# A decoder layer on one core: the last piece's residual in PSUM, transposes in a row, weights first, 4 KB store rows

## The chip, the core and the metric

The kernel runs on one core of a Trainium2 chip. A core has five engines with a queue of instructions each, executed in order: TensorE (PE; matmuls, written to PSUM; a matmul's stationary operand is loaded by a separate step, shown as PEld), VectorE (DVE), ScalarE (ACT), GpSimd (POOL), and SyncE (SP), which only issues DMA transfers here. The engines wait for each other through semaphores. Sixteen DMA engines move data between HBM and SBUF; the queues of SP and ACT feed them. The metric is the time of one execution on the device in microseconds.

## The reference, cut to what matters

One hybrid decoder layer in float32, batch 1, 256 positions, width 2048: retention and an RG-LRU side by side with a gated merge, cross-attention to 256 memory tokens, a gated feed-forward part with a causal convolution, a last RMSNorm. The parts that the change touches:

```python
h = h + memory_cross_attention(hn, mem_n, xa_w_q, xa_w_k, xa_w_v, xa_w_o)   # ends with o @ xa_w_o
hn = rmsnorm(h, norm_ffn_w)
h = h + conv_gated_ffn(hn, ffn_w_up, ffn_conv_w, ffn_conv_b, ffn_w_down)    # silu(gate) * val @ ffn_w_down, width 5632
return rmsnorm(h, final_norm_w)          # y * rsqrt(mean(y*y) + 1e-6) * w
```

Every matrix product is done with float32 operands split into a high part `hi` (float32r, rounded) and a low part `lo` (the rest), as hi*hi + lo*hi + hi*lo, so three matmuls stand for one.

## The kernel before

**Gemms.** All weights lie in one array, `wall`, in the order in which they are used. A gemm makes 512 output columns (a block, `b`) for all 256 rows. Its weights come in chunks of four 128-row tiles, 1 MB each (512 KB for the first ones: `EARLY`, sizes 2, 2, 4, 4, 4 for the first two gemms, which take turns). `prefetch` (L237) asks for the next chunk (a DMA by `load`, L191, at L192) into one of three raw buffers and records its split: `hi` by ACT (L283; by DVE, L281, for the very first piece), `lo` by DVE (L284), in halves of two tiles (`KH`), for the first two pieces in single tiles. `chunks` (L296) takes a chunk from the list `ahead` and calls `prefetch(AHEAD)`, which fills the list up to two. Each chunk of four tiles is 24 matmuls (two row blocks `tt` x four tiles x three products) through `mm` (L222). The activations `s` of the first gemms come from `x_t` through the class `Pairs` (ACT L429, DVE L430).

**Order.** The program is recorded by a framework that schedules each engine's queue by priorities and puts in the semaphores. Matmuls stay in the order of the program; a DMA that is "pinned" (`tc.keep_in_program_order`) does too. A tile that is written waits for those who still use it.

**Turning a block.** After a gemm, a block is turned by DMA (`by_dma`, L364): ACT copies the words into two 16-bit planes `pl` (L372), one for each `tt`; SP issues a transposing DMA for each into `pt` (L373); later ACT joins the halves into `f` (L383), and `split_cols` makes from it the operands `s` of the next gemm. `residual` (L792) does this for the four blocks of `w_mix_out` and of `xa_w_o`: residual add into `hrow[b]` (L804), turning, and sums of squares (L822). After `xa_w_o` comes the first gemm of the feed-forward part, whose last chunk needs the turned block 3.

**The end.** `down` (L949) runs the last gemms with `ffn_w_down`: blocks 0 to 2 as above, each finished by `finish` (squares into `ss3` by ACT, product with the norm weight by DVE). Block 3 is `last_down` (L964), per row block `tt` of 128 rows. For `tt` = 0 it is one sum of 512 columns, for `tt` = 1 two sums of 256 columns, `c` = 0 and 1 (36 matmuls each); they use two PSUM tiles, `accs[0]` and `accs[1]`. Each half is added to the residual (L989), squared and summed by DVE (L991). To have only one column left at the end, the sum of what is known after `c` = 0 (L996, L997) goes through a power of 0.5 on POOL (L998) into column 512 of `last`, behind the half `c` = 1, and is squared with it. A second power, of -0.5, gives the row's scale `r` (L1000). Then ACT and DVE scale the four blocks (L1008, L1004, L1010), and four stores of 128 rows x 2 KB go out (L1012), three by SP's queue, one by ACT's. `WARM` (L35) is the number of matmuls on constants before the first weights arrive (L219).

Of the kernel before, what the change touches and what calls it, by code (L numbers as in the profile page):

```python
# [17 lines left out]
P = 128  # L18
# [15 lines left out]
AHEAD = 2  # L34
WARM = 8  # L35
FREE = 300
# [9 lines left out]
C_INVF, C_SIGN, C_DEC = 0, 1, 2  # L46
C_WIDTH = C_DEC + HEADS * S


def constants():  # L50
# [8 lines left out]
    for h in range(HEADS):  # L59
        lg = np.log1p(-(2.0 ** (-5.0 - h)))  # L60
        dec = np.where(rel >= 0, np.exp(lg * np.maximum(rel, 0.0)), 0.0) * DK**-0.5
        c[:, C_DEC + h * S : C_DEC + (h + 1) * S] = dec
    return c

# [72 lines left out]
def hybrid_layer(  # L137
# [98 lines left out]

    def prefetch(n):  # L237
        while len(ahead) < n and taken[0] < len(stream):
# [13 lines left out]
            cuts = range(nk + 1) if i == 0 else range(0, nk + 1, KH) if i < 6 else (0, nk)  # L252
            if own:
                xs.load(k2 + 1)
            for a, b in zip(cuts, cuts[1:]):
                load(raw[:, a:b, :], src[:, a:b, :], early)
                if i == 0 and a == 0:
                    load(*xs.rest, early)
                elif own and a == 0:
                    xs.load(k2 + nk // KH)  # L260
# [12 lines left out]
            for k in range(0, nk, KH):  # L273
# [3 lines left out]
                lo = wp.tile([P, KH, BW], F32R, tag="lo", bufs=PART_BUFS, name=nm("lo"))  # L277
                for cs in (slice(k, k + 1), slice(k + 1, k + 2)) if i < 2 else (slice(k, k + KH),):
                    ds = slice(cs.start - k, cs.stop - k)
# [16 lines left out]
    def chunks(nk, w, row, c):  # L296
# [4 lines left out]
        for k, n in pieces(i, nk):  # L301
            prefetch(1)
            (r_, c_), parts = ahead.pop(0)
            assert (r_, c_) == (row + k * P, c)
            prefetch(AHEAD)
            yield k, n, parts
            step[0] += 1
            due = [p for p in pending if p[0] <= step[0]]
            pending[:] = [p for p in pending if p[0] > step[0]]
            for _, fn in due:  # L310
                fn()
# [51 lines left out]

    def by_dma(rows, then, wait=1):  # L364

# [4 lines left out]
        for tt in range(2):  # L370
            with tc.high_priority(FREE):
                act.copy(planes[:, tt], words[:, tt])  # L372
            sp.dma_start_transpose(  # L373
                out=turned_.rearrange("p h f s -> p (h f) s")[:, :, tt * P : (tt + 1) * P],
                in_=planes[:, tt].rearrange("p h n -> p (h n)"),
            )

        def join():
# [413 lines left out]
    def residual(w, st, out, wcol, steps=None):  # L792
# [3 lines left out]
        for b in range(4):  # L796
            if steps:
                steps(b)
            if b == 0:
                for one in products[:2]:  # L800
                    for _ in range(NT // KC - 1):
                        next(one)
            h = hrow[b]
            dve.tensor_add(h, h, ended(products[b]))  # L804
            by_dma(h, lambda f, b=b: turn(f, b, out, wcol), 1 + (b == 1))
            if b < 2:
# [157 lines left out]
    def last_down(b0, hid, n, b):  # L964
# [3 lines left out]
        dve.memset(half, 0.5)  # L968
        accs = [acc(), acc()]
        parts = [p for _, _, ps in chunks(n, "ffn_w_down", b0 * BW, b * BW) for p in ps]  # L970

        def total(o, tt, cs):
            for k in range(n):
                hi, lo = (t[:, k % KH, cs] for t in parts[k // KH])
                for _ in products_n(o, hid[k // 2][:, k % 2, :], hi, lo, tt, k == 0, k == n - 1):
                    pass

        for tt in range(2):
# [4 lines left out]
            for c in range(2):  # L983
                cs = slice(c * S, (c + 1) * S)
                o = accs[c][:, 1, 0:S] if tt else accs[0][:, 0, cs]
                if tt:
                    total(o, tt, cs)
                y = last[:, c * S : (c + 1) * S + c]
                dve.tensor_add(last[:, cs], h[:, tt, cs], o)  # L989
                junk = tp.tile([P, S + 1], F32, tag="tr", bufs=2, name=nm("junk"))  # L990
                dve.scalar_tensor_tensor(  # L991
                    out=junk[:, 0 : S + c], in0=y, scalar=1.0 / D if c else 1.0, in1=y, op0=ALU.mult, op1=ALU.mult,
                    accum_out=ss3[:, tt, b + c : b + c + 1],
                )
                if c == 0:
                    dve.tensor_reduce(out=before, in_=ss3[:, tt, 0:4], axis=AX.X, op=ALU.add)  # L996
                    dve.tensor_scalar_add(before, before, EPS * D)  # L997
                    pool.tensor_tensor(out=last[:, BW : BW + 1], in0=before, in1=half, op=ALU.pow)  # L998
            r = sp_.tile([P, 1], F32, tag="ro", bufs=5, name=nm("ro"))
            pool.tensor_tensor(out=r, in0=ss3[:, tt, 4:5], in1=mhalf[:, 0:1], op=ALU.pow)  # L1000
            for c in (1, 0, 3, 2):
                y = hrow[c][:, tt, :]
                if c == 3:
                    dve.scalar_tensor_tensor(  # L1004
                        out=y, in0=last[:, 0:BW], scalar=r, in1=wfin[1][:, 1, :], op0=ALU.mult, op1=ALU.mult
                    )
                elif c == 1:
                    dve.tensor_scalar_mul(y, y, r)  # L1008
                else:
                    act.mul(y, y, r)  # L1010
                queue = act if c == 2 else sp
                queue.dma_start(out=out[0, tt * P : (tt + 1) * P, c * BW : (c + 1) * BW], in_=y)  # L1012

# [10 lines left out]
    for kind, b, *n in ff_plan():  # L1024
# [6 lines left out]
        else:  # L1031
            final = b + n[0] == NF // 4
            if final:
                wfin = []
                for i in range(2):
# [40 lines left out]
```

## Time and profile before

| | us |
|---|---|
| three runs: lowest, median, highest | 2005.92, 2006.1, 2006.18 |
| the profiled execution: its time | 2006.16 |
| its span, first to last instruction | 2004.2 |
| PE busy in the span | 1993.6 |
| ACT busy, DVE busy | 1270.2, 1268.9 |
| DMA queue of SP: share of the 16 engines' span | 64.3% |

The span is what the views count in; the execution's time is 1.96 us longer. A row of a view gives the start, the time, the engine, the line of the kernel, the operation, what is written and from what (with partitions x elements), how many, and in brackets how long the engine was idle before it and who released it. Matmuls overlap in the pipeline: two rows of "0.39" can start 0.23 apart. A merged row ("x2", "x574") goes from the first start to the last end. SPq and ACTq are the issuing of a DMA; "to landing" is from the start of the issue to the last byte's arrival.

### The profile page before, as it was taken

The numbers are of one execution on the slowest core, as the hardware profiler recorded it, in microseconds if no ns is written. First come the engines' busy times: TensorE is split into PE (matmuls) and PEld (weight loads), VectorE is DVE, ScalarE is ACT, GpSimd is POOL, SyncE is SP. The second block draws the span as 40 slices with busy tenths as digits, with TensorE's granted clock in tenths as the row PEclk, the third lists the DMA queues.
The fourth block names the chain that finished last, engine by engine and source line by source line (L and its number), as shares of the span: only waits on it lengthen the run. The fifth ranks groups of instructions, "written<-read, shape, count | busy, mean of one in ns | idle before, by whom it ended". The sixth has DMA issues, their size and how long they took to land.

```text
span 2004.2 us, 23312 instructions
## 1 busy us (share of the span) xinstructions
PE 1993.6 (99%) x8924; PEld 1656.2 (83%) x8924; DVE 1268.9 (63%) x1566; ACT 1270.2 (63%) x1499; POOL 8.8 (0%) x14
## 2 busy tenths in 40 slices
PE   9999999999999999999999999999999999999998
PEld 7888888888888888888888888888888888888887
DVE  6857756888545555566555654667764576754775
ACT  6646548988444555587666666767763577734763
POOL 0000000000000000000000000000000000000000
PEclk9999999999999999999999999999999999999999
DMA  8755657665655556777666567767665577655673
GB/s 328 238 209 172 237 200 206 214 210 179 218 199 192 199 198 212 268 256 241 203 217 211 193 198 206 213 202 226 231 212 194 179 227 229 204 207 202 205 239 119
DMA packets 197904, 425.58 MB, mean 212 GB/s; under 512 B 142240, under 2 KB 146848, under 8 KB 152736
## 3 DMA queue, kind: packets, MB, share of 16 engines
q1 hardware_dynamic: 197360, 423.55, 64.3%
q8 instruction: 70, 1.15, 0.2%
q10 hardware_dynamic: 432, 0.53, 0.1%
q14 instruction: 42, 0.34, 0.0%
HBM read 388.39 MB, written 2.10 MB: 195 GB/s over the span
## 4 chain that ended last, share of the span: by engine, by line
PE 98%; DMA 1%; DVE 0%; ACT 0%; issue 0%; SPq 0%; POOLq 0%; POOL 0%
PE acc L222 96%; PE sm L222 2%; DMA pt<-pl 0%; DMA raw<-in_wall 0%; DVE lo L284 0%; ACT hi L283 0%; SPq L192 0%; ACT pl L372 0%; ACT nat L1010 0%; DVE last L989 0%; DVE nat L804 0%; ACT junk L822 0%; POOLq L1072 0%; POOL last L998 0%; DVE junk L991 0%
## 5 line engine op out<-in xcount | busy, mean ns | idle before, releaser
L222 PE MATMUL acc<-hi,s 128*128 128x512 f32 x5720 | 1757.7, 389 | 1.2 <-DVE last L989 0.8
L222 PEld LDWEIGHTS acc<-hi,s 128*128 128x128 f32 x5720 | 1071.7, 188 | 222.0 <-DVE last L989 1.3
L284 DVE TENSOR_TENSOR lo<-raw,hi 128x1024 fp32r<-128x1024 f32 (+1 forms) x714 | 859.7, 1220 | 596.9 <-ACT hi L283 579.4
L222 PE MATMUL acc<-lo,s 128*128 128x512 f32 x2860 | 1110.0, 388 | 0.5 <-DVE lo L284 0.5
L283 ACT CAST hi<-raw 128x1024 fp32r<-128x1024 f32 (+1 forms) x712 | 734.5, 1050 | 469.4 <-PE acc L222 427.3
L222 PEld LDWEIGHTS acc<-lo,s 128*128 128x128 f32 x2860 | 537.0, 188 | 112.1 <-DVE lo L284 1.3
L383 ACT COPY f<-pt 128x1024 uint16<-128x1024 uint16 x128 | 168.9, 1353 | 99.9 <-DMA pt<-pl 99.9
L372 ACT COPY pl<-rows 128x1024 uint16<-128x1024 uint16 x100 | 99.7, 1045 | 55.2 <-DVE rows L396 42.9
L396 DVE TENSOR_SCALAR rows<-acc,ro 128x512 f32<-128x512 f32 x76 | 53.4, 744 | 6.2 <-PE acc L222 6.2
L917 DVE SCALAR_TENSOR_TENSOR fg<-f,pf,fg 128x255 f32<-128x255 f32 (+1 forms) x88 | 37.4, 479 | 29.7 <-ACT fg L915 29.3
L917 DVE SCALAR_TENSOR_TENSOR fv<-f,pf,fv 128x255 f32<-128x255 f32 (+1 forms) x88 | 36.1, 478 | 3.9 <-ACT fv L915 3.8
L915 ACT ACTIVATE fg<-f,pf 128x256 f32<-128x256 f32 x44 | 22.9, 592 | 0.3
L915 ACT ACTIVATE fv<-f,pf 128x256 f32<-128x256 f32 x44 | 23.1, 592 | 0.0
L729 DVE SCALAR_TENSOR_TENSOR xr<-f,pa,xr 128x255 f32<-128x255 f32 (+2 forms) x48 | 20.2, 480 | 3.4 <-ACT xr L727 3.3
L404 DVE TENSOR_TENSOR s<-f,s 128x512 fp32r<-128x512 f32 x24 | 15.5, 687 | 9.9 <-ACT s L403 9.9
L430 DVE SCALAR_TENSOR_TENSOR s<-f,pb,s 128x256 fp32r<-128x256 f32 x48 | 20.1, 480 | 2.2 <-ACT s L429 2.2
L372 ACT COPY pl<-nat 128x1024 uint16<-128x1024 uint16 x16 | 15.9, 1045 | 7.5 <-DVE nat L804 7.5
L429 ACT ACTIVATE s<-f,pb 128x256 fp32r<-128x256 f32 x48 | 20.6, 503 | 0.0
L222 PEld LDWEIGHTS sm<-s,s 128*128 128x128 f32 x144 | 18.8, 191 | 0.9
L222 PE MATMUL sm<-s,s 128*128 128x256 f32 (+1 forms) x144 | 18.6, 279 | 0.0
L935 ACT ACTIVATE ft<-fg 128x512 f32<-128x512 f32 x22 | 13.9, 632 | 7.3 <-DVE fg L917 7.3
L418 ACT ACTIVATE v<-acc,ro 128x512 fp32r<-128x512 f32 x16 | 11.0, 686 | 10.2 <-DVE v L419 10.2
(137 smaller groups left out, 561.3 us busy)
## 6 DMA issues: line engine op xcount, KB each, us to landing
raw<-in_wall SPq DMA_DIRECT2D x352, 1024.0 KB, 4.9
nat<-in_x SPq DMA_DIRECT2D x8, 512.0 KB, 8.7
raw<-in_wall SPq DMA_DIRECT2D x7, 512.0 KB, 8.6
pt<-pl SPq DMA_TRANSPOSE x128, 3.3
nat<-in_mem SPq DMA_DIRECT2D x4, 512.0 KB, 8.4
xt<-in_x_t SPq DMA_DIRECT2D x3, 512.0 KB, 10.2
xt<-in_mem_t SPq DMA_DIRECT2D x3, 512.0 KB, 4.9
out<-nat SPq DMA_DIRECT2D x6, 256.0 KB, 2.9
```

What stands on the lines that cost most here:

```text
L222: tc.keep_in_program_order(pe.matmul(*a, **k))
L283: act.copy(hi[:, ds], raw[:, cs, :])
L284: dve.tensor_tensor(out=lo[:, ds], in0=raw[:, cs, :], in1=hi[:, ds].bitcast(F32), op=ALU.subtract)
L372: act.copy(planes[:, tt], words[:, tt])
L383: act.copy(halves_[:, :, :, cs], turned_[:, :, :, cs])
L396: dve.tensor_scalar_mul(rows[:, tt, :], a[:, tt, :], r[:, tt : tt + 1])
L404: dve.tensor_tensor(out=t[:, :, S:BW], in0=src, in1=t[:, :, 0:S].bitcast(F32), op=ALU.subtract)
L429: act.activation(t[:, j, 0:S], src[:, j, :], AF.Identity, scale=wcol(j))
L430: dve.scalar_tensor_tensor(out=t[:, j, S:BW], in0=src[:, j, :], scalar=wcol(j), in1=t[:, j, 0:S].bitcast(F32), op0=ALU.mult, op1=ALU.subtract,
L729: dve.scalar_tensor_tensor(out=y[:, s:S], in0=z[:, 0 : S - s], scalar=p_cw(3 - s, t), in1=y[:, s:S], op0=ALU.mult, op1=ALU.add,)
L915: act.activation(y, z[:, j, :], AF.Identity, scale=pf[:, 2, t : t + 1], bias=pf[:, 3, t : t + 1])
L917: dve.scalar_tensor_tensor(out=y[:, s:S], in0=z[:, j, 0 : S - s], scalar=pf[:, 2 - s, t : t + 1], in1=y[:, s:S], op0=ALU.mult, op1=ALU.add,)
```

## The change

The edits:

- the first weight piece is asked for ahead of the first tiles of `x_t`; `WARM` goes from 8 to 7; pieces three and four are split in single tiles, as the first two were;
- for the last block of `xa_w_o` (`hold`), the first three chunks are multiplied first; while the last chunk is taken, `held` keeps `chunks` from calling `prefetch`; both transposes are pinned; then `prefetch(AHEAD, True)` asks for the next chunk, pinned;
- the constants get an identity matrix, loaded ahead of the last part and copied to `one`; the half `c` = 1 of `tt` = 1 of the residual is split into `known` (high and low part), and two matmuls add it to the sum in PSUM ahead of the 36 others (`more`);
- this half's square comes from PSUM by ACT with the sum of squares, over 257 columns: the known sum's root is copied by ACT into column 256 of the same PSUM tile, ahead of that tile's matmuls in the program;
- three PSUM tiles instead of two, so that each sum has its own;
- the product with the norm weight is done for each half of block 3 by DVE (from PSUM for the last), ahead of the scaling;
- scaled blocks are written side by side in pairs into a raw buffer; two stores per row block, with rows of 4 KB, both by SP.

```diff
--- before.py
+++ after.py
@@ -32,7 +32,7 @@
 RAW_BUFS = 3
 PART_BUFS = 6
 AHEAD = 2
-WARM = 8
+WARM = 7
 FREE = 300
 RG_WAIT = 3
 EPS = 1e-6
@@ -44,7 +44,8 @@
 O_XR, O_YR, O_GA, O_GB = 6144, 8192, 10240, 12288
 
 C_INVF, C_SIGN, C_DEC = 0, 1, 2
-C_WIDTH = C_DEC + HEADS * S
+C_ID = C_DEC + HEADS * S
+C_WIDTH = C_ID + P
 
 
 def constants():
@@ -60,6 +61,7 @@
         lg = np.log1p(-(2.0 ** (-5.0 - h)))
         dec = np.where(rel >= 0, np.exp(lg * np.maximum(rel, 0.0)), 0.0) * DK**-0.5
         c[:, C_DEC + h * S : C_DEC + (h + 1) * S] = dec
+    c[:, C_ID:] = np.eye(P)
     return c
 
 
@@ -234,7 +236,9 @@
 
     at = [0]
 
-    def prefetch(n):
+    held = [False]
+
+    def prefetch(n, pin=False):
         while len(ahead) < n and taken[0] < len(stream):
             i = taken[0]
             name, row, nk, c = stream[i]
@@ -250,11 +254,12 @@
             early = i < 2 * len(EARLY)
             own = early and i % 2 == 0
             cuts = range(nk + 1) if i == 0 else range(0, nk + 1, KH) if i < 6 else (0, nk)
-            if own:
+            if own and i > 0:
                 xs.load(k2 + 1)
             for a, b in zip(cuts, cuts[1:]):
-                load(raw[:, a:b, :], src[:, a:b, :], early)
+                load(raw[:, a:b, :], src[:, a:b, :], early or pin)
                 if i == 0 and a == 0:
+                    xs.load(1)
                     load(*xs.rest, early)
                 elif own and a == 0:
                     xs.load(k2 + nk // KH)
@@ -275,7 +280,7 @@
                     xs[k2 + k // KH]
                 hi = wp.tile([P, KH, BW], F32R, tag="hi", bufs=PART_BUFS, name=nm("hi"))
                 lo = wp.tile([P, KH, BW], F32R, tag="lo", bufs=PART_BUFS, name=nm("lo"))
-                for cs in (slice(k, k + 1), slice(k + 1, k + 2)) if i < 2 else (slice(k, k + KH),):
+                for cs in (slice(k, k + 1), slice(k + 1, k + 2)) if i < 4 else (slice(k, k + KH),):
                     ds = slice(cs.start - k, cs.stop - k)
                     if i == 0:
                         dve.tensor_copy(hi[:, ds], raw[:, cs, :])
@@ -302,7 +307,8 @@
             prefetch(1)
             (r_, c_), parts = ahead.pop(0)
             assert (r_, c_) == (row + k * P, c)
-            prefetch(AHEAD)
+            if not held[0]:
+                prefetch(AHEAD)
             yield k, n, parts
             step[0] += 1
             due = [p for p in pending if p[0] <= step[0]]
@@ -361,7 +367,7 @@
 
         return t[:, j, cs], t[:, j, S + cs.start : S + cs.stop]
 
-    def by_dma(rows, then, wait=1):
+    def by_dma(rows, then, wait=1, pin=False):
 
 
         planes = big([P, 2, 2, BW], U16, s="pl")
@@ -370,10 +376,12 @@
         for tt in range(2):
             with tc.high_priority(FREE):
                 act.copy(planes[:, tt], words[:, tt])
-            sp.dma_start_transpose(
+            turning = sp.dma_start_transpose(
                 out=turned_.rearrange("p h f s -> p (h f) s")[:, :, tt * P : (tt + 1) * P],
                 in_=planes[:, tt].rearrange("p h n -> p (h n)"),
             )
+            if pin:
+                tc.keep_in_program_order(turning)
 
         def join():
             f = big([P, 4, S], s="f")
@@ -801,8 +809,16 @@
                     for _ in range(NT // KC - 1):
                         next(one)
             h = hrow[b]
+            hold = b == 3 and steps is None
+            if hold:
+                for _ in range(NT // KC - 1):
+                    next(products[b])
+            held[0] = hold
             dve.tensor_add(h, h, ended(products[b]))
-            by_dma(h, lambda f, b=b: turn(f, b, out, wcol), 1 + (b == 1))
+            by_dma(h, lambda f, b=b: turn(f, b, out, wcol), 1 + (b == 1), hold)
+            if hold:
+                held[0] = False
+                prefetch(AHEAD, True)
             if b < 2:
                 later(2 + b, lambda h=h, b=b: squares(h, ss, b))
             else:
@@ -966,13 +982,22 @@
         h = hrow[b]
         half = sp_.tile([P, 1], F32, tag="half", bufs=1, name="half")
         dve.memset(half, 0.5)
-        accs = [acc(), acc()]
+        accs = [acc() for _ in range(3)]
+        one = tp.tile([P, P], F32R, tag="tr", bufs=2, name="one")
+        dve.tensor_copy(one, unit[0][:, 0, 0:P])
+        rest = h[:, 1, S:BW]
+        known = big([P, 2, S], F32R, s="h")
+        act.copy(known[:, 0, :], rest)
+        dve.tensor_tensor(out=known[:, 1, :], in0=rest, in1=known[:, 0, :].bitcast(F32), op=ALU.subtract)
         parts = [p for _, _, ps in chunks(n, "ffn_w_down", b0 * BW, b * BW) for p in ps]
 
-        def total(o, tt, cs):
+        def total(o, tt, cs, more=False):
+            if more:
+                for i in range(2):
+                    mm(o, one, known[:, i, :], start=i == 0, stop=False)
             for k in range(n):
                 hi, lo = (t[:, k % KH, cs] for t in parts[k // KH])
-                for _ in products_n(o, hid[k // 2][:, k % 2, :], hi, lo, tt, k == 0, k == n - 1):
+                for _ in products_n(o, hid[k // 2][:, k % 2, :], hi, lo, tt, k == 0 and not more, k == n - 1):
                     pass
 
         for tt in range(2):
@@ -982,34 +1007,45 @@
                 total(accs[0][:, 0, :], tt, slice(0, BW))
             for c in range(2):
                 cs = slice(c * S, (c + 1) * S)
-                o = accs[c][:, 1, 0:S] if tt else accs[0][:, 0, cs]
+                o = accs[1 + c][:, 0, 0:S] if tt else accs[0][:, 0, cs]
                 if tt:
-                    total(o, tt, cs)
-                y = last[:, c * S : (c + 1) * S + c]
-                dve.tensor_add(last[:, cs], h[:, tt, cs], o)
+                    total(o, tt, cs, c == 1)
+                if tt and c:
+                    y, z = accs[2][:, 0, 0 : S + 1], o
+                else:
+                    y, z = last[:, c * S : (c + 1) * S + c], last[:, cs]
+                    dve.tensor_add(z, h[:, tt, cs], o)
                 junk = tp.tile([P, S + 1], F32, tag="tr", bufs=2, name=nm("junk"))
-                dve.scalar_tensor_tensor(
-                    out=junk[:, 0 : S + c], in0=y, scalar=1.0 / D if c else 1.0, in1=y, op0=ALU.mult, op1=ALU.mult,
-                    accum_out=ss3[:, tt, b + c : b + c + 1],
-                )
+                if tt and c:
+                    act.activation(
+                        junk, y, AF.Square, scale=float(D**-0.5), accum_out=ss3[:, tt, b + c : b + c + 1]
+                    )
+                else:
+                    dve.scalar_tensor_tensor(
+                        out=junk[:, 0 : S + c], in0=y, scalar=1.0 / D if c else 1.0, in1=y, op0=ALU.mult, op1=ALU.mult,
+                        accum_out=ss3[:, tt, b + c : b + c + 1],
+                    )
                 if c == 0:
                     dve.tensor_reduce(out=before, in_=ss3[:, tt, 0:4], axis=AX.X, op=ALU.add)
                     dve.tensor_scalar_add(before, before, EPS * D)
                     pool.tensor_tensor(out=last[:, BW : BW + 1], in0=before, in1=half, op=ALU.pow)
+                    if tt:
+                        act.copy(accs[2][:, 0, S : S + 1], last[:, BW : BW + 1])
+                dve.tensor_tensor(out=last[:, cs], in0=z, in1=wfin[1][:, 1, cs], op=ALU.mult)
             r = sp_.tile([P, 1], F32, tag="ro", bufs=5, name=nm("ro"))
             pool.tensor_tensor(out=r, in0=ss3[:, tt, 4:5], in1=mhalf[:, 0:1], op=ALU.pow)
-            for c in (1, 0, 3, 2):
-                y = hrow[c][:, tt, :]
-                if c == 3:
-                    dve.scalar_tensor_tensor(
-                        out=y, in0=last[:, 0:BW], scalar=r, in1=wfin[1][:, 1, :], op0=ALU.mult, op1=ALU.mult
-                    )
-                elif c == 1:
-                    dve.tensor_scalar_mul(y, y, r)
-                else:
-                    act.mul(y, y, r)
-                queue = act if c == 2 else sp
-                queue.dma_start(out=out[0, tt * P : (tt + 1) * P, c * BW : (c + 1) * BW], in_=y)
+            scaled = wp.tile([P, 4, BW], F32, tag="raw", bufs=RAW_BUFS, name=nm("out"))
+            rows = [hrow[c][:, tt, :] for c in range(3)] + [last[:, 0:BW]]
+            for c in range(2):
+                dve.tensor_scalar_mul(scaled[:, 2 * c, :], rows[2 * c], r)
+                late = S if c else 0
+                act.mul(scaled[:, 2 * c + 1, late:], rows[2 * c + 1][:, late:], r)
+                if late:
+                    dve.tensor_scalar_mul(scaled[:, 3, 0:late], rows[3][:, 0:late], r)
+                sp.dma_start(
+                    out=out[0, tt * P : (tt + 1) * P, 2 * c * BW : 2 * (c + 1) * BW],
+                    in_=scaled[:, 2 * c : 2 * c + 2, :].rearrange("p c n -> p (c n)"),
+                )
 
     ss3 = sp_.tile([P, 2, 5], F32, tag="ss3", bufs=1, name="ss3")
 
@@ -1031,7 +1067,8 @@
         else:
             final = b + n[0] == NF // 4
             if final:
-                wfin = []
+                wfin, unit = [], [tmp("unit")]
+                sp.dma_start(out=unit[0][:, 0, 0:P], in_=consts[:, C_ID:])
                 for i in range(2):
                     t = big([P, 2, BW], s="wf")
                     sp.dma_start(
```

## The prediction

> **What bounds the kernel now.** I read the page first, then what TensorE (PE) waited for, then the chain of work that ended last.
>
> ```profile
> span 2004.2 us, 23312 instructions
> PE 1993.6 (99%) x8924; PEld 1656.2 (83%) x8924; DVE 1268.9 (63%) x1566; ACT 1270.2 (63%) x1499; POOL 8.8 (0%) x14
> ...
> PE warm L219 <- DVE half L968: 1.1, 1, 1.1
> PE acc L222 <- DVE last L989: 0.8, 1, 0.8
> PE acc L222 <- DVE lo L284: 0.5, 1, 0.5
> PE acc L222 <- DVE s L430: 0.4, 1, 0.4
> ```
>
> PE is idle for 2004.2 - 1993.6 = 10.6 us: 1.1 before its first matmul, three waits (0.8, 0.5, 0.4), and the rest, 7.8 us, after its last matmul. Nothing else can be gained without removing matmuls. The change goes at all three waits and at the tail. The price of a late matmul is read from the chain:
>
> ```profile
> 9.90 1.06 ACT hi L283
> ...
> 12.27 130.41 PE acc L222 x574
> ...
> 1987.45 4.58 PE acc L222 x36
> ```
>
> 574 matmuls of 512 columns in 130.41 us are 0.227 us each; 36 of 256 columns in 4.58 us are 0.12 each, with some 0.1 to fill the pipeline after a stop. Between the stops PE never waits, so what makes it stop costs its full length. Times below are on the clock of this execution, before any shift.
>
> **The start.** These rows stand around the first wait.
>
> ```profile
> 4.73 1.77 PE L222 MATMUL acc<-hi,s 128*128 128x512 f32 x4
> 6.34 0.62 PE L222 MATMUL acc<-lo,s 128*128 128x512 f32 x2
> 7.24 1.15 ACT L283 CAST hi<-raw 128x512 fp32r<-128x512 f32 x2 [2.32 <-DMA raw<-in_wall]
> 7.90 1.29 DVE L284 TENSOR_TENSOR lo<-raw,hi 128x512 fp32r<-128x512 f32 x2 [0.77 <-ACT hi L283]
> 10.98 2.48 DVE L284 TENSOR_TENSOR lo<-raw,hi 128x1024 fp32r<-128x1024 f32 x2 [0.96 <-ACT hi L283]
> 11.04 0.70 PE L222 MATMUL acc<-hi,s 128*128 128x512 f32 x2
> 12.27 0.50 PE L222 MATMUL acc<-lo,s 128*128 128x512 f32 x1 [0.53 <-DVE lo L284]
> ```
>
> The third weight piece lands at 9.9; ACT casts its whole 128x1024 half (1.06), DVE subtracts it (1.24), and PE's first lo matmul, due at 11.04 + 2 x 0.227 = 11.50, starts at 12.27. The change does the third and fourth pieces in 128x512 steps (0.57 ACT, 0.65 DVE by the 7.24 and 7.90 rows): 9.90 + 0.57 + 0.65 = 11.1, before 11.50. The wait of 0.77 goes, and with it 0.1 of refill: -0.9. What is late next is the second half, ready at about 11.8 and due at 12.2. Weights first and one warm matmul less move only what comes before 7.24: the second product's piece lands in the same place of the queue behind the same bytes, and its cast at 7.24 sets the later matmuls. I take 0 for them; bounds for the whole start are 0 (the halves come late after all) and -1.5 (that piece lands 0.6 earlier too).
>
> **The turn into the feed-forward part.** Here lies most of my sum.
>
> ```profile
> 1261.37 0.51 SPq L192 DMA_DIRECT2D raw<-in_wall  x1
> ...
> 1275.63 0.39 PE L222 MATMUL acc<-lo,s 128*128 128x512 f32 x1
> 1276.70 1.22 DVE L804 TENSOR_TENSOR nat<-nat,acc 128x1024 f32<-128x1024 f32 x1
> 1277.94 2.00 ACT L372 COPY pl<-nat 128x1024 uint16<-128x1024 uint16 x2 [1.06 <-DVE nat L804]
> 1279.02 1.25 SPq L373 DMA_TRANSPOSE pt<-pl  x1
> 1281.75 0.39 PE L222 MATMUL acc<-lo,s 128*128 128x512 f32 x1
> 1288.95 1.35 ACT L383 COPY f<-pt 128x1024 uint16<-128x1024 uint16 x1 [2.43 <-DMA pt<-pl]
> 1291.12 1.70 ACT L429 ACTIVATE s<-f,pb 128x256 fp32r<-128x256 f32 x4
> 1292.92 0.50 PE L222 MATMUL acc<-hi,s 128*128 128x512 f32 x1 [0.36 <-DVE s L430]
> ...
> DMA to landing us min/median/max: 3.0/3.3/8.0
> ...
> DMA to landing us min/median/max: 2.8/4.9/12.7
> ```
>
> (The last two rows are the transposes and the weight loads. The 1275.63 row ends the residual's last sum.) The first gemm of the feed-forward part uses four weight chunks. PE starts chunk 0 at 1275.85, chunk 1 24 matmuls later (its first lo at 1281.75), and at chunk 3 it waits for the turned last block, 0.5 with the refill; that block was slow because its second transpose is the 8.0 of the transposes' row: it shared the engines with weight loads. With the change, `held` skips the prefetch when the last chunk of the residual is taken, and chunk 1 is asked for behind both transposes, pinned. In the built program's SP queue the load of chunk 1, issued at 1261.37 before, stands directly behind the second transpose of the last block, and ACT's cast of it stands behind the two copies `f` and the four `s` of that block. So PE will wait for it:
>
> - Residual add at 1276.1 (its sum ends then, and DVE has no subtraction of chunk 1 ahead of it any more) to 1277.3; first copy `pl` to 1278.35, second to 1279.3.
> - Transposes issued at 1278.4 and 1279.7 (1.25 each), the load of chunk 1 at 1281.0. They land at 1281.5, 1282.8 and (4.9) 1285.9.
> - ACT: `f` to 1282.8 and 1284.2, `s` until 1285.7; cast of chunk 1 at 1285.9 to 1287.0, DVE's lo to 1288.2, PE's lo at 1288.3.
>
> That is 6.5 after 1281.75, and 0.1 of refill. The old wait of 0.5 goes, since the block is split by 1286. Chunks 2 and 3 land 2.6 apart (about half of a load's 4.9 is transfer) and PE needs 5.5 for each: no further wait. Net +6.1. Bounds: a load that lands as soon as ACT is free gives +5.7; one delayed like the transposes (8 instead of 4.9) gives +9, but the queue holds nothing else then, so I allow 1.9: +8.0.
>
> A stop of this length has a second price, the clock.
>
> ```profile
> 1996.06 0.28 PE L222 MATMUL acc<-lo,s 128*128 128x256 f32 x1
> ...
> 1996.40:1999.40 3.00, 0.00 (x0) 0.00 (x0) 1.98 (x5) 1.33 (x2) 0.55 (x1) 1.00 0.02 6
> 1999.50:2002.00 2.50, 0.00 (x0) 0.00 (x0) 0.00 (x0) 0.00 (x0) 0.00 (x0) 0.50 1.06 355
> ```
>
> The third figure from the end of a window's row is the granted clock: full until 1999.4, half after it, some 3.1 us after the last matmul ended at 1996.34. And at the start, with PE at work since 1.05, four matmuls took from 4.73 to 6.34, 0.40 each, and those after 6.34 go at 0.227. PE stands from 1281.5 to 1287.0, 5.5 us, so I expect the half clock, and 5.3 us of it (1.05 to 6.34) after the restart. Of these 1.2 are the wait for lo anyway; the other 4.1 do 0.227/0.40 of their work: +1.8. Bounds: 0 (the clock stays) and +2.5.
>
> The Trainium skill, "TensorE: Matmul & The Clock Gate", section "Part 1: The HAM clock gate (the "warmup" mystery)", says that the array falls to half rate after one idle window of about 3.4 us and comes back after one busy window, and that the windows run freely. The two rows above agree with it. By that rule a stop of 5.5 us holds a whole window only in (5.5 - 3.4) / 3.4 = 6 of 10 runs, an estimate from the page; it speaks for the rival below in which this term is 0.
>
> **The last piece.** PE's old wait at 1987.45 shows how PSUM tiles are tracked: it writes the other half of a tile that DVE still reads, and waits.
>
> ```profile
> 1987.45 0.50 PE L222 MATMUL acc<-hi,s 128*128 128x256 f32 x2 [0.84 <-DVE last L989]
> ...
> 1991.86 0.40 PE L222 MATMUL acc<-hi,s 128*128 128x256 f32 x2
> ...
> 1990.03 0.49 DVE L1008 TENSOR_SCALAR nat<-nat,ro 128x512 f32<-128x512 f32 x1 [0.67 <-POOL ro L1000]
> 1992.06 0.42 DVE L989 TENSOR_TENSOR last<-nat,acc 128x256 f32<-128x256 f32 x1 [0.88 <-PE acc L222]
> 1993.17 0.15 DVE L997 TENSOR_SCALAR pt<-pt 128x1 f32<-128x1 f32 x1
> 1993.54 0.54 POOL L998 TENSOR_TENSOR last<-pt,half 128x1 f32<-128x1 f32 x1 [3.55 <-DVE pt L997]
> 1996.37 0.42 DVE L989 TENSOR_TENSOR last<-nat,acc 128x256 f32<-128x256 f32 x1 [3.05 <-PE acc L222]
> 1997.25 0.08 DVE L991 DVE_READ_ACCUMULATOR junk<-last 128x1 f32 x1
> 1997.41 0.55 POOL L1000 TENSOR_TENSOR ro<-ss,mhalf 128x1 f32<-128x1 f32 x1 [3.33 <-DVE junk L991]
> 1999.36 0.36 ACTq L1012 DMA_DIRECT2D out<-nat  x1
> ```
>
> With its own tile the second row block starts at 1986.45, and its first 36 matmuls end at 1991.0 instead of 1992.0. But the third tile gets, ahead of its matmuls, the square root of the sum so far, copied in by ACT as a 257th column; tracked as a whole, that tile makes PE's residual matmuls wait for the copy, as the built program has it. So the last 38 matmuls, which followed without a stop at 1991.86, now stand behind this: DVE is busy with the first row block until 1991.4 (a multiplication by the weights ahead of its first power puts the scale 0.3 behind the 1990.03 row, and three scalings follow, 0.4 + 0.4 + 0.35); add, square, reduction and the new multiplication take until 1992.9 (1.1 from add to the 1993.17 row, and 0.26 for the multiplication between); the power ends at 1993.5; a one-column copy, some 0.25, 1993.8. Start +2.0; the two residual matmuls 0.24 and the refill: last matmul ends at 1998.65, +2.3. ACT's square of 257 columns straight from PSUM, about 0.5 (an estimate: ACT's 512 columns took 0.57, and a short read of the sum follows), replaces add and square on DVE (1996.37 to 1997.33, 0.96): the second power starts 1.9 later. Scaling is about as long as before, ending 1.7 later. The stop of some 2.8 us is shorter than the 3.1 above, so I leave the clock full there; it would cost another 38 x 0.12 = 4.6.
>
> **The stores** have the same 1 MB per row block in two transfers instead of four. The last of four was issued when ACT's and DVE's scalings ended (the 1999.36 row); now the first goes at about 2000.6 and the second at 2001.1. I take the same rate: +1.7 for the whole tail, bounds +0.9 (longer rows move faster, DVE not late) and +2.3.
>
> **Costed at nothing:** the load of the identity, its copy, and the split of the residual into two (one ACT and two DVE instructions of up to 0.5). Both engines idle 37% of the span and the nearest waits come tens of microseconds later; on PE's path they would cost 0.5.
>
> **Sum:** -0.9 + 6.1 + 1.8 + 1.7 = +8.7 on 2004.2, so 2012.9 span. This execution took 2006.16, 1.96 more than its span, and lies on the median 2006.1: 2014.8.
>
> **Rivals.**
>
> 1. The clock stays full through the stop: +6.9, 2013.0. For it: the window may not fall whole into the stop. Against: the fall 3.1 us after the last matmul.
> 2. The clock falls in the last piece too: +13.3, 2019.4. For it: 2.8 is near 3.1. Against: it is shorter, and matmuls run on both sides.
> 3. The held load costs nothing, and the change is not slower: -0.9 - 0.5 + 1.7 = +0.3, 2006.4. It decides at 1278.9: chunk 1 must land by then for cast and lo to be done by 1281.75, 2 us before SP is free of the transposes. Against it stand the queue's order and the single prefetch; for it only that the old wait was really there.
> 4. As 3, and PE does not wait for the copied column either, so that the residual's sum in PSUM does what it says: the piece ends 0.8 earlier, the square saves 0.45: tail -1.4, total -2.8, 2003.3. Against: the wait at 1987.45.
>
> **Chances:** forecast 0.66, rival 1 0.20, rival 2 0.08, rival 3 0.04, rival 4 0.02. Within 0.2% (about 4 us, what a measurement here tells from no change) lie rival 3 and most of 4: faster 0.01, same 0.05, slower 0.94. The range takes rival 1 with its bounds below and the dearer load and clock above: 2012.2 to 2017.3.
>
> **What would show it.** In the changed profile PE has no wait for lo L289 near 12; a wait of 5 to 7 us for ACT's hi or DVE's lo around 1281 to 1288, with the load of that piece issued right after two transposes; matmuls of 0.4 behind it and a granted clock below 1; a wait of 2 to 3 us for ACT's copy L1033 near the end. I am wrong if the load stands ahead of the transposes, if PE goes through 1281 without a stop, or if the last 38 matmuls follow at once.

## The result, and the profile after

The changed kernel takes 2017.84 us (median of 6 runs, 2016.55 to 2018.35), the kernel before beside it 2006.1 (2005.92 to 2006.25): a ratio of 1.0057, 95% interval 1.0045 to 1.007, or +11.7 us. The forecast was 2014.8 with a range up to 2017.3: slower, as it said, but by 3 us more, and above the range. The profiled execution took 2018.17, with a span of 2016.2.

First the page of the changed kernel (span; busy time of each engine), then the table of what PE waited for (total, times, longest):

```profile
span 2016.2 us, 23317 instructions
...
PE 1998.6 (99%) x8924; PEld 1660.4 (82%) x8924; DVE 1269.9 (63%) x1573; ACT 1269.3 (63%) x1505; POOL 9.0 (0%) x14
```

```profile
PE acc L224 <- ACT hi L288: 6.1, 1, 6.1
PE acc L224 <- ACT acc L1033: 3.0, 1, 3.0
PE warm L221 <- DVE half L984: 1.1, 1, 1.1
PE acc L224 <- ACT s L437: 0.7, 1, 0.7
```

The two large waits are the forecast ones: the held load (ACT's hi, 6.1) and the copied root (L1033, 3.0). The 0.7 for ACT's `s` is new: the first real matmul waits for its activations, now that `x_t` is asked for behind the first weights. But the span grew by 12.0, and PE's idle time only from 10.6 to 17.6. The other 5.0 stand in PE's *busy* time: 1998.6 instead of 1993.6 for the same number of matmuls, 8924 (two fewer to warm up, two more for the residual). Matmuls that are longer without being more are matmuls at a lower clock.

Where that is shows in the timeline of the changed kernel (start, duration, then what; in brackets the idle time before and who ended it):

```profile
5.07 2.32 PE L224 MATMUL acc<-hi,s 128*128 128x512 f32 x4 [0.67 <-ACT s L437]
...
8.04 1.91 PE L224 MATMUL acc<-hi,s 128*128 128x512 f32 x4
...
9.75 0.72 PE L224 MATMUL acc<-lo,s 128*128 128x512 f32 x2
10.30 0.63 PE L224 MATMUL acc<-hi,s 128*128 128x512 f32 x2
...
13.73 0.62 PE L224 MATMUL acc<-hi,s 128*128 128x512 f32 x2
...
1279.48 2.61 SPq L379 DMA_TRANSPOSE pt<-pl  x2
...
1282.18 17.57 SPq L194 DMA_DIRECT2D raw<-in_wall  x7
...
1287.54 1.99 ACT L288 CAST hi<-raw 128x1024 fp32r<-128x1024 f32 x2 [0.52 <-DMA raw<-in_wall]
...
1288.63 1.22 PE L224 MATMUL acc<-hi,s 128*128 128x512 f32 x2 [6.08 <-ACT hi L288]
...
1289.89 0.80 PE L224 MATMUL acc<-lo,s 128*128 128x512 f32 x1
...
2002.92 0.16 ACT L1033 COPY acc<-last 128x1 f32<-128x1 f32 x1 [2.12 <-POOL last L1031]
...
2003.14 0.65 PE L224 MATMUL acc<-h,one 128*128 128x256 f32 x2 [3.01 <-ACT acc L1033]
...
2009.16 0.28 PE L224 MATMUL acc<-lo,s 128*128 128x256 f32 x1
...
2010.08 0.54 POOL L1036 TENSOR_TENSOR ro<-ss,mhalf 128x1 f32<-128x1 f32 x1 [7.19 <-ACT junk L1020]
...
2011.40 0.81 SPq L1045 DMA_DIRECT2D out<-out  x2
```

Four matmuls from 8.04 to 9.75 are 0.43 each, and only from about 10 on 0.23 (the trace's record of the granted clock turns full at 9.94). Before, matmuls took 0.227 from 6.34 on, and the record turned full at 6.04. The turn has two transposes in a row, the load behind them, and the cast only when it has landed. In the windows of the same trace (start and end, length, busy time of PE, PEld, DVE, ACT, POOL with instructions, then granted clock, DMA share, GB/s) the clock falls twice:

```profile
1286.60:1293.30 6.70, 4.63 (x10) 3.26 (x11) 5.40 (x7) 5.11 (x7) 0.00 (x0) 0.50 0.90 357
1293.40:1296.00 2.60, 2.60 (x13) 2.13 (x12) 2.47 (x3) 1.25 (x3) 0.00 (x0) 1.00 1.00 381
...
2003.40:2006.70 3.30, 3.30 (x17) 3.30 (x17) 0.00 (x0) 0.00 (x0) 0.00 (x0) 0.50 0.15 57
2006.80:2009.40 2.60, 2.60 (x22) 2.43 (x21) 0.00 (x0) 0.00 (x0) 0.00 (x0) 1.00 0.00 0
```

Following one matmul through both traces gives the account of the 12.0. The same matmul (the 28th after the warm ones) starts at 12.60 before and at 13.73 now: the start has cost 1.1. Behind the turn the distance is 9.2, at the first matmul of the last piece's second row block 8.2, at the residual's 11.3, at the last matmul 13.1, at the end of the span 12.0.

| part | forecast | trace |
|---|---|---|
| start | -0.9 | +1.1 |
| turn, with its clock | +6.1 +1.8 = +7.9 | +8.1 |
| last piece up to its last matmul | +2.3 | +3.9 |
| from there to the end (square, power, scaling, stores) | -0.6 | -1.1 |
| sum | +8.7 | +12.0 |

### The profile page after: what moved, and what is told of

It reads as the page before. It is cut to its first block, busy times and chain, and to the rows that moved or that the text cites. A ratio compares the mean times of both kernels' runs of the same rounds, so it can differ in the third digit from the quotient of the medians.

```text
span 2016.2 us, 23317 instructions
## 1 busy us (share of the span) xinstructions
PE 1998.6 (99%) x8924; PEld 1660.4 (82%) x8924; DVE 1269.9 (63%) x1573; ACT 1269.3 (63%) x1505; POOL 9.0 (0%) x14
## 4 chain that ended last, share of the span: by engine, by line
PE 98%; DMA 0%; issue 0%; DVE 0%; ACT 0%; POOL 0%; SPq 0%; POOLq 0%; DVEq 0%; ACTq 0%
PE acc L224 96%; PE sm L224 2%; DMA raw<-in_wall 0%; DMA xt<-in_x_t 0%; ACT pl L378 0%; DVE out L1040 0%; DVE junk L1024 0%; ACT junk L838 0%; DVE nat L817 0%; POOL last L1031 0%; DVE last L1017 0%; ACT hi L288 0%; POOL ro L1036 0%; DVE last L1034 0%; POOLq L1109 0%
## 5 line engine op out<-in xcount | busy, mean ns | idle before, releaser
L412 DVE TENSOR_TENSOR s<-f,s 128x512 fp32r<-128x512 f32 x24 | 15.5, 687 | 10.6 <-ACT s L411 10.6
L426 ACT ACTIVATE v<-acc,ro 128x512 fp32r<-128x512 f32 x16 | 10.9, 682 | 10.2 <-DVE v L427 10.2
## 6 DMA issues: line engine op xcount, KB each, us to landing
xt<-in_x_t SPq DMA_DIRECT2D x3, 512.0 KB, 10.2
```

Of the source, the lines that this page charges most:

```text
L412: dve.tensor_tensor(out=t[:, :, S:BW], in0=src, in1=t[:, :, 0:S].bitcast(F32), op=ALU.subtract)
```

## The experiments

Each run was timed beside the kernel before on its own chip: 2006.66 (27 runs, 2005.4 to 2007.58) for the first four, 2006.25 (21 runs) for the next four, 2006.45 (21 runs) for the last four. These chips scatter more than the first: an interval of 0.0009 to either side is 1.8 us, so differences below 2 us are left to the traces, where the distance of one matmul from the same matmul of the kernel before is read to 0.1, but for one execution each.

One thing about the trace of the kernel before has to be known for this. Its wait for the turned block near 1292.9, which holds up the matmuls behind it by 0.6, does not appear in the traces of `start_all`, `start_split`, `piece_free`, `best` and `warm_4`, which leave the turn as it was; in those of `piece_only` and `best_warm` half of the 0.6 appears. So that wait belongs to that execution and not to the kernel, and distances from the kernel before that are read behind the turn hold up to 0.6 that is no edit's work.

**The parts alone**

`start_all`:

```
-WARM = 8
+WARM = 7
-            if own:
+            if own and i > 0:
...
+                    xs.load(1)
...
-  ... if i < 2 else (slice(k, k + KH),):
+  ... if i < 4 else (slice(k, k + KH),):
```

> The kernel before with the edits of the start alone: weights requested first, 7 warm matmuls, the third and fourth pieces split in 128x512 steps. In the changed kernel's trace the granted clock turned full at 9.94 us (6.04 before) and the matmuls of the start ran 1.1 us later in the end. Theory A (the clock opens one window of 3.41 later, because PE has a hole of 0.66 between its last warm matmul and its first real one): full clock again near 9.9, +1.1, so 2007.2. Theory B (the prediction: only the split counts, the clock of the changed run was chance): full clock near 6.0, -0.9, so 2005.2. If the window falls by chance, the runs scatter between the two by 2.

Measured 2006.27 (2005.79 to 2007.76), ratio 0.9998 (0.9989 to 1.0007). Its trace, PE's timeline:

```profile
5.16 2.26 PE L222 MATMUL acc<-hi,s 128*128 128x512 f32 x4 [0.75 <-ACT s L430]
...
8.07 1.87 PE L222 MATMUL acc<-hi,s 128*128 128x512 f32 x4
9.77 0.62 PE L222 MATMUL acc<-lo,s 128*128 128x512 f32 x2
```

The slow matmuls until 9.77 are there without any other part of the change, and in that execution the 28th matmul is 1.05 late: the trace is theory A's. The time does not decide: its interval, -2.2 to +1.4 us, holds both.

`start_split` has the last of these edits alone.

> The kernel before with the split of the third and fourth pieces alone; 8 warm matmuls and the old order of the loads. Both theories: PE does not wait for lo L284 near 12.27 any more, full clock near 6.0, -0.9: 2005.2. If the split itself makes the start slower (ACT and DVE have four instructions more), it is not below 2006.1.

Measured 2005.07 (2004.66 to 2007.68), ratio 0.9994 (0.9985 to 1.0003), so some 1.2 less, but not told from no change. In its trace the wait for lo is gone and the 28th matmul starts 0.5 earlier than before (the rest of the 1.2 by which its span is shorter is the turn's wait). The forecast -0.9 belongs to this edit; it was the other two that were taken for nothing.

`hold_only` has the held prefetch and the pinned transposes of the diff (and the identity in the constants, which nothing reads here):

> The kernel before with the held prefetch and the pinned transposes alone. Theory (as predicted, and as the changed kernel's trace shows: the matmuls behind the turn run 8.1 later): chunk 1 of the first feed-forward gemm is loaded behind two transposes, PE stands 6, the clock halves for two windows: +8.1, 2014.2; a run whose clock stays full would take 2.5 less, 2011.7. Rival (the stop is made worse by the edits of the start, which shift the clock's windows): +6.2, 2012.3 in all runs.

Measured 2014.71 (2013.84 to 2015.5), ratio 1.0038 (1.0026 to 1.0051): +8.05, as expected. In its trace PE waits 5.7 for the cast and the turn costs 7.6; the clock halves for the same 6.83. The rival falls by the trace (the interval, +5.2 to +10.2, holds its +6.2 too): no edit of the start is needed for the halved clock. In the trace the load stands directly behind both transposes (issued at 1281.70, they at 1278.99), and PE waits for its cast. No run has the hold and the pins apart.

`piece_only` has the last piece, the stores and the constants:

> The kernel before with the last piece, its PSUM tiles, the stores and the constants alone. Theory A (as in the changed kernel's trace): PE waits 3.0 for ACT's copy of the root, the clock halves for one window in the last piece, and the tail behind the last matmul is 1.1 shorter: +2.0 +1.8 -1.1 = +2.7, 2008.8. Theory B (the prediction: the clock stays full): +2.0 +0.3 -1.1 = +1.2, 2007.3, or with the stores as slow as before +1.7, 2007.8. If the halved window is a matter of phase, runs of both kinds appear, 1.5 apart.

Measured 2009.89 (2008.15 to 2010.75), ratio 1.0015 (1.0006 to 1.0023): +3.2, nearer to A's +2.7 than to B's +1.2 or +1.7, though the interval (1.2 to 4.6 us) holds them all. Its trace began with a start that was 1.8 late by itself (in these traces even starts without an edit lie 0.3 to 1.8 behind the one of before), and then does what A says. Windows of this trace:

```profile
1991.80:1995.10 3.30, 0.60 (x6) 0.40 (x4) 2.46 (x9) 1.12 (x2) 0.59 (x2) 1.00 0.48 194
1995.30:1998.60 3.30, 3.18 (x15) 3.18 (x16) 0.00 (x0) 0.07 (x1) 0.00 (x0) 0.50 0.26 101
```

In the 3.3 us ahead of the fall PE was at work for 0.6: the window was not empty, and the clock fell all the same. The runs may be of two kinds, as the expectation says of a matter of phase: the six with a mean granted clock of 0.998 have a median of 2010.2, the five with 0.999 one of 2008.7. That is a hint and not proof, since this mean is rounded and also counts the half clock behind the last matmul.

**PE kept at work in the stops**

`after_busy` is the changed kernel with unused products ahead of the two waiting matmuls (`fill` has their numbers, counted from 0, and how many products go ahead of each); the waits themselves stay:

```
+    calls, fill = [0], {5696: 18, 8840: 8}
     def mm(*a, **k):
+        if calls[0] in fill:
+            idle = px.tile([P, 2, S], F32, tag="sm", name=nm("sm"))
+            for _ in range(fill[calls[0]]):
+                tc.keep_in_program_order(pe.matmul(idle[:, 0, 0:P], ones, ones, start=True, stop=True))
+        calls[0] += 1
         tc.keep_in_program_order(pe.matmul(*a, **k))
```

> The changed kernel, with PE kept at work in its two stops: 18 unused matmuls of ones ahead of the matmul that waits for chunk 1, and 8 ahead of the residual's matmuls in the last piece. The stops themselves stay. Theory A (behind a stop the halved clock is paid for as well: 2.5 in the turn and 1.6 in the last piece, by the changed kernel's trace): the granted clock is full in both places, the matmuls behind them go at 0.227 and 0.12 at once, and the time is 4.1 less than the changed kernel's +11.7 over before: +7.6. Theory B (the slow matmuls behind a stop come from something else than PE's idleness): the same +11.7.

Measured 2016.74 (2014.47 to 2017.04), ratio 1.0051 (1.0038 to 1.0063): +10.5, between the theories. Its windows tell why:

```profile
1285.40:1288.70 3.30, 1.41 (x9) 0.78 (x7) 2.58 (x5) 3.14 (x5) 0.00 (x0) 1.00 1.01 420
1288.80:1292.10 3.30, 3.04 (x7) 2.46 (x8) 3.07 (x4) 2.33 (x3) 0.00 (x0) 0.50 0.89 318
1998.80:2002.20 3.40, 2.17 (x20) 1.98 (x19) 2.36 (x9) 1.18 (x3) 0.54 (x1) 1.00 0.57 230
2002.20:2005.60 3.40, 3.40 (x28) 3.40 (x29) 0.00 (x0) 0.00 (x0) 0.00 (x0) 1.00 0.20 78
```

In the last piece 8 products kept the clock; the residual still waits 1.2 for the copy, and the matmuls behind it go at 0.12. In the turn 18 were not enough: a stretch of 3.3 with 1.41 of work still lost the clock, for one window instead of two. One run of the five took only 2014.47, with a mean granted clock of 0.999 where the others have 0.998; it may have kept the clock.

`after_full` fills the turn with 24 and starts with 10 warm matmuls (`WARM = 10`, `{5696: 24, 8840: 8}`); `after_again` is the changed kernel unaltered beside it.

> The changed kernel once more, unaltered, so that the next run has it beside it on one chip. As measured: +11.7 over before. If the windows of the clock fall by chance, its granted clock is full from another moment than 9.94, and the total moves by up to 2.

> The changed kernel with PE kept at work at all three places: 10 warm matmuls, 24 unused matmuls (18 left the clock to fall for one window) in the turn's stop, 8 in the last piece's. Theory A (the clock's three terms are what the prediction lacks): granted clock full from 6 to the end; the start +0.2, the turn +5.9, the piece and the stores +1.2: +7.3 over before, 4.4 below the changed kernel beside it. Theory B (only the clock in the turn counts): +9.5 or more.

Measured 2017.64 (2017.19 to 2018.22), ratio 1.0057 (1.0043 to 1.007), and 2013.93 (2013.76 to 2014.28), ratio 1.0039 (1.0026 to 1.0051): +11.2 and +7.5, with no run of the one near a run of the other. Windows of the filled kernel:

```profile
1282.00:1288.00 6.00, 5.28 (x47) 5.09 (x46) 1.91 (x5) 5.43 (x8) 0.07 (x1) 1.00 1.02 353
1288.80:1296.00 7.20, 6.95 (x31) 5.75 (x32) 6.06 (x6) 5.08 (x6) 0.00 (x0) 1.00 0.95 357
...
2003.00:2006.00 3.00, 2.52 (x22) 2.31 (x20) 0.00 (x0) 0.40 (x2) 0.00 (x0) 1.00 0.00 0
```

Full clock throughout. Compared matmul by matmul with `after_again`, it gains 0.9 in the start, 1.6 in the turn and 1.5 in the last piece, 4.0 of the traces' distance, 3.7 of the medians'. So theory A holds: work that produces nothing makes the kernel 3.7 us faster, since the matmuls behind it run at full clock.

**The start once more**

`after_warm` is the changed kernel with `WARM = 10`, `warm_4` the kernel before with `WARM = 4`.

> The changed kernel with 10 warm matmuls instead of 7 (before: 8), so that PE has no hole between them and the first real one. Theory A (the hole of 0.66 behind the seventh lets the clock's window pass, full only at 9.94): full clock by 6.5, the start 2 earlier, the time 2 less: +9.7 over before, and less scatter. Theory B (the window's phase or the late first product decides): full clock near 9.9 still in some runs, +11 to +12.

> The kernel before with 4 warm matmuls instead of 8 and nothing else. Theory A (a hole ahead of the first real matmul keeps the clock half for a window more): the warm matmuls end near 3.0, the first real one starts at 4.7 as before, full clock one window of 3.41 later (8 to 10 instead of 4 to 6), and the 8 to 15 matmuls in between at 0.43 instead of 0.227: +1.5 to +2.5. Theory B (what counts is the load order, not the warm matmuls): no change.

Measured 2017.23 (2015.81 to 2017.82), ratio 1.0054 (1.0042 to 1.0067), so +11.0, and 2006.67 (2005.68 to 2008.06), ratio 1.0002 (0.9993 to 1.001). Both of theory A's sizes were missed, and by the times alone theory B is nearer in both. The clock did roughly what A says: with 10 it was full at 6.04, with 4 only at 7.65. But little came of it. `after_warm`, PE's timeline:

```profile
7.13 1.07 PE L224 MATMUL acc<-hi,s 128*128 128x512 f32 x4
8.04 0.61 PE L224 MATMUL acc<-lo,s 128*128 128x512 f32 x2
8.99 0.73 PE L224 MATMUL acc<-hi,s 128*128 128x512 f32 x2 [0.34 <-ACT hi L288]
```

PE is quick at 7.13, and then stands for the next weight piece. The start is bound by what lands, so that of the 2 us which the clock takes there about half comes back as a wait when the clock is full. In `warm_4` it is the other way round: PE runs slowly until 7.65, the old wait for lo is 0.4 shorter, and the 28th matmul is 0.1 late.

**A version without the copy**

`piece_free` has the last piece and the stores of the change, but the root is not put into PSUM; the rest of the sum is added to the square's:

```
-                    y, z = accs[2][:, 0, 0 : S + 1], o
+                    y, z = o, o
...
-                    if tt:
-                        act.copy(accs[2][:, 0, S : S + 1], last[:, BW : BW + 1])
+                    if tt:
+                        dve.tensor_scalar_mul(before, before, 1.0 / D)
...
+                elif tt:
+                    dve.tensor_add(ss3[:, tt, 4:5], ss3[:, tt, 4:5], before)
```

`best` adds the split (`i < 4`), `best_warm` also `WARM = 10`.

> The last piece alone (as before with nothing else changed), but without the root in PSUM: the tile has 256 columns, ACT squares them, and the rest of the sum is added by DVE (128x1) ahead of the second power, so PE's residual matmuls wait for nothing. Theory (the wait for ACT's copy is what the piece costs): no stop in the last piece, clock full; -1.0 (own tile) +0.24 (two matmuls) -1.1 (the tail) +0.2 (the added sum) = -1.7 against before, 4.8 under the piece with the copy. Rival (the late start of the third tile comes from DVE, busy with the first row block): PE still waits 2 to 3, and the time is above before's.

> The same last piece without the root in PSUM, and the split of the third and fourth weight pieces; 8 warm matmuls, old order of the loads, no held prefetch. Theory: -0.9 -1.7 = -2.6 against before. If the scatter of the start hides the split, -1.7.

> The version with the last piece without the root in PSUM and the split (which measured 2.6 under before), now with 10 warm matmuls instead of 8. Theory A: the first real matmul starts up to 0.4 later (the warm ones end at 5.8 at half clock), and the clock is full by 6.5 whatever the phase of its windows: between 0.4 more and 0.5 less than with 8, with less scatter. If the window still passes sometimes, runs 2 above the others remain.

Measured: `piece_free` 2004.68 (2003.49 to 2005.47), ratio 0.9992 (0.9983 to 1.0); `best` 2003.63 (2002.92 to 2006.42), 0.999 (0.9981 to 0.9999); `best_warm` 2004.11 (2003.38 to 2005.15), 0.9988 (0.9979 to 0.9997). What PE waited for in `piece_free`:

```profile
PE warm L221 <- DVE half L983: 1.1, 1, 1.1
PE acc L224 <- DVE hi L285: 0.5, 1, 0.5
PE acc L224 <- DVE lo L288: 0.3, 1, 0.3
```

There is no stop in the last piece, so the rival (DVE busy with the first row block) falls: the copy alone made it. In its trace the second row block starts 1.1 earlier than before's by its own tile, the last matmul 0.9, the two residual matmuls taken off, and the tail is 0.9 shorter. `best` is 2.6 under the kernel before beside it and so beats both kernels; its interval just leaves out no change, as does that of `best_warm`. That the 2.6 is the forecast figure is in part luck: in the trace it is 0.1 from the start, 0.7 from the turn, which has no edit, 0.9 from the last piece and 0.9 from the tail. More warm matmuls did not show a gain: of the last two neither is told from the other.

## Why the forecast was right in direction and short in size

- **Turn: right.** The load of chunk 1 was issued directly behind both transposes at 1282.18, which is 1281.05 on the clock of before (the start's 1.1 taken off) against the 1281.0 worked out. It took 5.3 instead of 4.9, so the cast began at 1286.4 instead of 1285.9; PE's lo came 7.0 late instead of 6.5. The half clock behind it cost 1.7, from 1289.89 on, against 1.8. `hold_only` gives +8.05 for the whole against +7.9. Rivals 1, 3 and 4 are out: the clock fell, and nothing was hidden. Some luck is in the closeness: the old wait of 0.5, which the sum takes off, is missing in most of the other executions without the hold, so that against those the turn costs 0.6 more.
- **Last piece: the stop was right, the clock behind it wrong.** The own tile gave -1.1 (forecast -1.0), and the residual's matmul started 2.0 late, exactly as worked out. The step that failed reads "The stop of some 2.8 us is shorter than the 3.1 above, so I leave the clock full there". The 3.1 between the last matmul and the fall of the clock, in the trace of before, was taken for a least length of stop. It was the end of a window, in which PE had still worked for 0.3. All four profiled executions with this copy and no filling (the changed kernel twice, `after_warm`, `piece_only`) lost the clock in the stop of 3.0, for one window: 1.5, by `after_full` against `after_again`. Rival 2 had the event right and its price wrong: it let all 38 matmuls run at half clock (4.6), where one window of 3.4 ends it.
- **Start: the term for the split was right, the zero beside it wrong.** Up to the first lo of the third piece the matmuls are 1.9 behind those of before, from there on 1.1: the old wait is gone, 0.8 for the forecast 0.9. But "Weights first and one warm matmul less move only what comes before 7.24 [...] I take 0 for them" failed: it overlooked that these edits decide when the clock turns full, and its bounds for the start, 0 and -1.5, left no room for a loss. The warm matmuls ended at 4.41 and the first product came at 5.07 (4.73 before); with that hole the clock was full at 9.94, 9.76, 10.11 and 8.78 in the four executions with 7 warm matmuls, and at 6.04 and 5.02 in the two of the changed kernel with 10 instead. That is +2.0 against the forecast, of which 10 warm matmuls return 0.9. How much of the rest is the later first product and how much the chance of that execution stays open: unchanged starts differ by up to 1.8 between the traces, and the medians of `start_all` and before do not differ.
- **From the last matmul to the end: -1.1 instead of -0.6.** The second power starts 0.92 after the last matmul's start, before 1.35 (ACT squares out of PSUM at once, and no add stands ahead of it), and the two stores are issued within 1.8 of the power's start, before four within 2.0, and land 0.3 sooner after the last issue. "I take the same rate" was too cautious: in the middle of the last stores the rate is 400 to 410 GB/s, before 290 to 390. Whether the longer rows do this, as the lower bound has it, or the fewer transfers, was not tried apart.

The misses are +2.0 for the start, +1.5 for the clock in the last piece, +0.2 for the turn and -0.5 for the tail: +3.2 of the 3.3 between 8.7 and 12.0. The upper end of the range, 2017.3, has the dearer load and clock of the turn and nothing for the two terms that failed. (Its lower end does not follow from the bounds: rival 1 with -1.5, +5.7 and +0.9 is +5.1, which is 2011.2 and not 2012.2.)

The Trainium skill, "TensorE: Matmul & The Clock Gate", section "Why this matters for your kernels", advises against gaps over about 3 us between bursts of matmuls. The gap of 3.0 here bears it out. The reason given there, one window of idleness, does not fit as it stands: 1.41 of work in 3.3 did not keep the clock. The prediction says that its rows agree with the rule of a whole idle window, and takes from it 6 chances in 10 for a stop of 5.5. Its own row says otherwise: the fall 3.1 after the last matmul ended a window that was not wholly idle. And all 21 runs with the held load and without filling have a mean granted clock of 0.996 to 0.998, where each run of the kernel before beside the experiments has 0.999.

## What to carry to other kernels

A stop of the array costs its length and then the clock: cost every stop of 3 us or more with the half-speed matmuls behind it (here 1.5 to 1.7 us), and let unused products run in a stop that cannot be removed. Before a prefetch is moved behind other transfers of the same queue, add up the queue: two transposes of 1.3 us each to issue, a landing of 5.3 and a cast of 1.05 were more than one chunk's lead. A value written into a tile that the array is about to fill makes the array wait for the writer, even where the columns differ; add it afterwards instead.

## What had not been expected of the hardware

- The clock is judged in windows on a fixed grid: in the changed kernel it changed at 9.94, 1286.52, 1293.35, 2003.32 and 2006.74, and the distances 1276.58, 6.83, 709.97 and 3.41 are whole multiples of 3.413. The grid's place differs from execution to execution.
- A window need not be empty to lose the clock, and not full to win it. These are four windows of the grid, from `after_busy`, `warm_4`, `after` and `best` (the record of the clock begins with its first change, so that a row ahead of that shows 1.00 even at half clock):

```profile
1285.36:1288.77 3.41, 1.45 (x9) 0.82 (x7) 2.67 (x5) 3.18 (x5) 0.00 (x0) 1.00 1.01 420
1994.21:1997.62 3.41, 1.64 (x14) 1.44 (x12) 0.97 (x4) 0.12 (x1) 0.54 (x1) 1.00 0.00 0
3.11:6.53 3.42, 2.75 (x10) 1.98 (x9) 1.91 (x4) 0.91 (x2) 0.00 (x0) 1.00 0.95 313
0.47:3.88 3.41, 2.83 (x13) 2.83 (x14) 0.42 (x4) 2.08 (x3) 0.00 (x0) 1.00 0.50 154
```

The first lost the clock at its end, the second kept it (it fell only at 2001.03, behind an empty window). The third did not win the clock, the fourth did, at 3.88. All the windows of the fourteen traces fall on these sides: at full clock, up to 1.45 of work lost it and 1.64 or more kept it; at half clock, up to 2.75 left it half and 2.83 or more made it full. So 0.66 us without work kept the clock half in the start, where 0.58 did not.
- From this an estimate: a full-clock window bears between 3.41 - 1.64 = 1.77 and 3.41 - 1.45 = 1.96 us without work. A stop of 3.0 can lie across two windows so that neither has too much of it, at 16 to 27% of the positions of the grid; one longer than 3.9, twice 1.96, always costs the clock.
- At half clock matmuls count as busy time. A page on which PE's share stays at 99% can hide 5 us of lost time, as here; the count of matmuls and their mean duration show it.
